# Two parked expert groups per query tile, half weight tiles, a tenth row buffer and 85 parked groups in a one-core encoder block

## The chip, the cores and the metric

The kernel runs on one core of one Trainium2 chip. A core has a matrix engine (TensorE, in the profile PE, with its weight loads as PEld), VectorE (DVE), ScalarE (ACT), GpSimd (POOL) and SyncE (SP), which here only issues DMAs. Each engine works through its own queue in order; they meet at semaphores. The metric is the device time of one execution in microseconds (us).

## What is computed

One layer of an encoder on 1024 tokens of width 1024: attention and a bidirectional state-space mixer, merged by gates, and then an expert mixer (PEER) with 16384 experts. The change lies in the expert mixer:

```python
def peer(h, w_query, keys1, keys2, u_tab, v_tab):
    ...
        q = (xt @ w_query).reshape(T, PEER_HEADS, 2, PEER_D_HALF)
        s1 = jnp.einsum('thd,hkd->thk', q[:, :, 0], keys1).astype(jnp.float32)
        s2 = jnp.einsum('thd,hkd->thk', q[:, :, 1], keys2).astype(jnp.float32)
        v1, i1 = lax.top_k(s1, PEER_TOPK)
        v2, i2 = lax.top_k(s2, PEER_TOPK)
        cand = (v1[..., :, None] + v2[..., None, :]).reshape(...)
        sc, pos = lax.top_k(cand, PEER_TOPK)
        idx = jnp.take_along_axis(cidx, pos, axis=-1)
        g = jax.nn.softmax(sc, axis=-1)
        u = u_tab[idx]
        a = jax.nn.gelu(jnp.einsum('thkd,td->thk', u, xt).astype(jnp.float32))
        vv = v_tab[idx]
        return jnp.einsum('thk,thkd->td', (g * a).astype(vv.dtype), vv)
```

Every token picks 128 experts (8 heads of 16), takes the dot product of each expert's row of `u` with the token, a gelu and a gate, and adds up the same experts' rows of `v`.

## The kernel before

The kernel does the expert mixer in two ways at once. For the first `TB` = 384 tokens (three blocks of 128) it **fetches** the picked rows: `rows` (L1162) issues an indirect DMA from POOL that brings one row of 1024 numbers for each of 128 tokens into a buffer `br`; a row of `u` is met by a dot product on DVE (`dot`, L1189), four of `v` by matmuls with a diagonal of weights (`add`, L1229). For the other `TA` = 640 tokens it computes **all experts densely**: the 128 groups of 128 experts each give a hidden tile `a`, gelu of `u` group times tokens (`hidden_parts`, L1303), which is multiplied by a gate tile that is zero where an expert was not picked, and then by the group's rows of `v` (`mixed`, L1560).

All products of the dense part are made in three matmuls from a high and a low half of each operand (`mm3`, L192). `weights` (L178) loads a weight tile in two raw halves `wr` (three buffers, DMA from SP), casts each on ACT into `wh` and subtracts on POOL into `wl`. `wh` and `wl` are tiles of 8 x 128 columns with two buffers each. With a list `late`, the subtracts are put off until `lows` is called; for a while in the routing `halves_by` sends them to DVE.

The stages of the expert half, with their times in the profiled execution:

1. Query loop (L1421, from about 1420 us): for 16 query tiles, PE multiplies the later tokens by a slice of `w_query`, scores them against the keys, and then runs four parts, that is one tile, of `parking`: it computes the hidden tile of one group ahead of its gate and writes it to DRAM (`a_d`). Meanwhile DVE takes the top 16 of each score tile (`top`, five passes) and routes the first three blocks (`route`). As soon as the first block is routed (`early`), fetches begin.
2. The rest of the tops and routes (L1441 to L1463, to about 2150 us). `hide` runs parked parts on PE while DVE has planned work ahead, up to `4 * NPARK - HOLD` parts.
3. Placing (L1482, to about 2582 us): DVE compares indices four tokens at a time (`quad`, `GB` = 6 buffers), PE multiplies them into gate tiles, which go to DRAM (`G_d`). `hide` goes on parking.
4. The last loop (L1594, to about 4000 us): the 128 groups in 43 lots of `EG` = 3. For each lot the hidden tiles are computed or, if parked, read back from DRAM; they are multiplied by the gate tile (`weigh`), and the lot before is mixed.

The order of the instructions on PE, DVE and POOL in these stages is written out by the program as it runs (`manual`), on ACT and SP a scheduler chooses it. The program keeps three planned clocks, `at_pe`, `at_dve` and `at_dma`: `follow` and `hide` give work to the engine that is behind, and `feed` (L1356) issues row fetches until `at_dma` has caught up with the larger of the other two. Each fetch adds 1.6 to `at_dma`; a u row adds 1.25 to `at_dve`, a v row 0.46 to `at_pe`.

The fetches have `NROW` = 9 row buffers. `drain(keep)` (L1168) puts the dots or matmuls of earlier rows into their queues until at most `keep` rows are open, and then the next fetch is issued; `keep` is `NROW - 1`.

88 of the 128 groups are parked, spread evenly, so most lots hold two parked groups, two hold three, and the computed one may stand at any place in its lot.

`hidden_parts` goes through its two token halves j one after the other, with eight slices kd each; the refill of its weight tile is ordered at the end (`load`), and the subtracts of the refill ordered before are put in at the middle:

```python
        for j in range(NJ):
            ...
            for kd in range(8):
                mm3(o, (uh[:, kd], ul[:, kd]), (h2h[kd][:, js], h2l[kd][:, js]), kd == 0, kd == 7)
                done += 1
                if done == 4 * NJ:
                    lows()
                if done % (2 * NJ) == 0 and done < 8 * NJ:
                    yield None
            ACT.activation(a[:, js], o, AF.Gelu_apprx_tanh)
        load()
        yield a
```

Of the kernel before, what the change touches and what calls it, by code (L numbers as in the profile page):

```python
# [28 lines left out]
W2 = TA // NJ  # L29
CUTS = [(0, TQ)] + [(TQ + j * W2, W2) for j in range(NJ)]  # L30
EPS = 1e-6
NEG = -3.0e38
EG = 3
NPARK = 88
BSTEP = 3
FSTEP = 2
NROW = 9
VG = 4
# [9 lines left out]
NGQ = 2  # L48
GB = 6
RDVE = 1  # L50
# [8 lines left out]
NSTG = 2  # L59
WH = 2  # L60
WL = 2
VB = 3
# [56 lines left out]
def block(ctx, tc, A, out, dbg=None):  # L119
# [57 lines left out]

    def weights(src, kd, eng=None, late=None):  # L178
        hi = wp.tile([128, 8, 128], FR, name="wh", bufs=WH)
        lo = wp.tile([128, 8, 128], FR, name="wl", bufs=WL)  # L180
        for k in range(0, kd, 4):
            raw = wp.tile([128, 4, 128], F32, name="wr", bufs=WR)
            nc.sync.dma_start(raw, src[:, k:k + 4])
            if late is None:
                split(raw, hi[:, k:k + 4], lo[:, k:k + 4], eng and eng[k // 4])
                continue
            ACT.copy(hi[:, k:k + 4], raw)  # L187
            late.append(lambda k=k, raw=raw: ((eng and eng[k // 4]) or POOL).tensor_tensor(  # L188
                lo[:, k:k + 4], raw, f32(hi[:, k:k + 4]), op=OP.subtract))
        return hi, lo  # L190
# [605 lines left out]
    bidx = bp.tile([128, NB, 128], I32, name="bidx")  # L796
    bg = bp.tile([128, NB, 128], F32, name="bg")
    hx = pool("hx")
    la = pool("la")
# [155 lines left out]
    rt = pool("rt", "right")  # L955
    kr = rt.tile([128, N_KR], F32, name="kr")
    nc.sync.dma_start(kr, A["kr"])
    for nm, x in zip("hl", (xh, xl)):
        for p, a in zip(x, others(nm, FR)):
            p[1] = a  # L960
    h2h, h2l = ([x[m][1] for m in range(8)] for x in (xh, xl))
    ip = pool("ip", "right")
    bw = pool("bw", "right")
    best = [bw.tile([128, 4, 2, 8, 16], F32, name="best", bufs=2) for _ in range(2)]
    where = [bw.tile([128, 4, 2, 8, 16], U32, name="where", bufs=2) for _ in range(2)]
# [68 lines left out]
    def route(blk):  # L1034
# [66 lines left out]
        if blk < NB:  # L1101
            V.tensor_copy(bidx[:, blk], exf)
            V.tensor_copy(bx[:, blk], exf)
            V.tensor_copy(bg[:, blk], gf)
            ready.append(blk)
            yield
            return
        ei = T([128, 3, 128], "ri3", I32)
# [18 lines left out]
    def final(p, src, t0, n, x1):  # L1127
        tl = slice(t0, t0 + n)
        nc.sync.dma_start(x1, x1_d[:, :, tl])
        yield "w"  # L1130
        yield "w"
        yield "w"
        for m in range(8):
            V.scalar_tensor_tensor(x1[:, m], src[:, m // 4, m % 4], mod[:, 40 + m:41 + m], x1[:, m], op0=OP.mult, op1=OP.add)
        yield "w"
        o = wide()
        acc = o[:, 0]
        for m in range(0, 8, 2):
            some = []
            for _ in range(2):  # L1140
                some.append(p.tile([128, n], F32, name="fsq", bufs=2))
# [12 lines left out]
        nc.sync.dma_start(out[:, :, tl], x1)  # L1154

    def fetched():
# [5 lines left out]
        def rows(tab, idx):  # L1162
            r = rt.tile([128, D], F32, name="br", bufs=NROW)
            POOL.indirect_dma_start(out=r, out_offset=None, in_=A[tab],  # L1164
                                    in_offset=bass.IndirectOffsetOnAxis(ap=idx, axis=0))
            return r
# [5 lines left out]
        for b in range(NB):  # L1172
# [3 lines left out]
            aT = rt.tile([128, 128], F32, name="aT")  # L1176
            yield from drain(NROW - 1)
            st = rt.tile([128, D], F32, name="br", bufs=NROW)
            nc.sync.dma_start(st, h2t_d[b])
            hrow = []  # L1180
# [16 lines left out]

            def weights_of(b=b, a=a, aT=aT):
                ACT.activation(a, a, AF.Gelu_apprx_tanh)
                yield "w"  # L1200
                V.tensor_tensor(a, a, bg[:, b], op=OP.mult)
                yield "w"
                yield "w"
                yield "w"
                o = P1()
                PE.transpose(o[:, :128], a, ident)
                ACT.copy(aT, o[:, :128])

            ahead.append((1, begin))
            for s in range(128):  # L1210
                yield from drain(NROW - 1)
                r = rows("u", bidx[:, b, s:s + 1])
                ahead.append((1, lambda s=s, r=r, dot=dot: dot(s, r)))
                if s == 96:
# [5 lines left out]
            def add(i, R, aT=aT, acc=acc):  # L1220
                if not acc:
                    acc.append(wide())
                z = zb[i // VG % 2]
                if i % VG == 0:
                    ACT.copy(z[:, :, 31:31 + 32 * VG:32], aT.rearrange("p (g i) -> p g i", g=4)[:, :, i:i + VG])
                at = 31 + 32 * (i % VG) - i
                for h in range(2):
                    for g in range(4):
                        PE.matmul(acc[0][32 * g:32 * g + 32, h], lhsT=z[:, g, at:at + 32], rhs=R[g][:, h * 512:(h + 1) * 512],  # L1229
                                  start=(i == 0), stop=(i == 31))  # L1230
                return
                yield

            def finish(b=b, acc=acc):
                s = rt.tile([128, D], F32, name="bacc")
# [5 lines left out]
                for m in range(8):  # L1241
                    PE.transpose(o[:, m // 4, m % 4], s[:, m * 128:(m + 1) * 128], ident)
                x1 = rt.tile([128, 8, 128], F32, name="bacc")
                yield from final(rt, o, b * 128, 128, x1)

            for i in range(32):
                R = []
                for g in range(4):
                    yield from drain(NROW - 1 - g)
                    R.append(rows("v", ixt[:, 32 * g + i:32 * g + i + 1]))  # L1250
                    yield "v"
# [24 lines left out]
    lt.release()  # L1276
    la.release()
    dn = pool("dn")
# [13 lines left out]

    def load():
        lows()
        src = next(sources, None)
        if src is not None:
            loaded.append(weights(src, 8, halves_by, late))

    load()
    load()  # L1300
    lows()

    def hidden_parts(c):  # L1303
        uh, ul = loaded.popleft()
        a = dn.tile([128, TA], F32, name="a", bufs=2)
        done = 0
        for j in range(NJ):
            o = psE.tile([128, 512], F32, name="hb", bufs=2)[:, :W2]
            js = slice(j * W2, (j + 1) * W2)
            for kd in range(8):  # L1310
                mm3(o, (uh[:, kd], ul[:, kd]), (h2h[kd][:, js], h2l[kd][:, js]), kd == 0, kd == 7)
                done += 1
                if done == 4 * NJ:
                    lows()
                if done % (2 * NJ) == 0 and done < 8 * NJ:
                    yield None
            ACT.activation(a[:, js], o, AF.Gelu_apprx_tanh)  # L1317
        load()
        yield a

# [100 lines left out]
    for m in range(17):  # L1421
# [15 lines left out]
        if m < 16:  # L1437
            for _ in range(4):
                parked_part()
# [189 lines left out]
    for m in range(8):  # L1629
        x1 = rt.tile([128, TA], F32, name="br", bufs=NROW)  # L1630
        nc.sync.dma_start(x1, x1_d[:, m, TB:])
# [3 lines left out]
    def last(m, j, js, o):  # L1635
        x = acc[:, m, js]
        V.scalar_tensor_tensor(x, o, mod[:, 40 + m:41 + m], x, op0=OP.mult, op1=OP.add)
        sq = rt.tile([128, W2], F32, name="br", bufs=NROW)
        ACT.activation(sq, x, AF.Square)
# [12 lines left out]
    d2.release()  # L1652
    dn.release()
    hx.release()
    bp.release()
# [63 lines left out]
```

## Time and profile before

| | |
|---|---|
| three runs | 4056.01, 4068.97 and 4076.5 us, median 4068.97 |
| the profiled execution | 4056.31 us |
| its span, from first to last instruction | 4054.5 us |
| mean granted PE clock | 0.953 |
| moved by DMA | 854.04 MB, mean 211 GB/s |
| row fetches | 384 of u and 384 of v, 402.70 MB on POOL's queue |
| hidden tiles | 128, of 48 matmuls (128x128 by 128x320) each |

The page gives for each engine the time in which it ran instructions; for a stage, a table by stretches gives the same with the clock that PE was granted. A stage whose PE column is short of its length has PE waiting, and the list of waits names the instruction that waited and the one that released it. A line like `wl L188 <- ACT wh L187` reads: the instruction of line 188 that writes `wl` stood idle until ACT's instruction of line 187 was done. SP's own timeline shows when each DMA was issued.

### The profile page before, as it was taken

The page shows a single profiled execution, that of the slowest core. Times are in us where ns is not written, and L with a number is a line of the kernel's source. Part 1 is how long each engine was busy: PE and PEld are TensorE (multiplying, and loading weights), DVE is VectorE, ACT ScalarE, POOL GpSimd, SP SyncE. Part 2 cuts the span into 40 slices and gives each one's busy share as a digit, 9 for nine tenths or more (in the row PEclk, how much of TensorE's full clock was granted, in tenths as well). Part 3 has the DMA queues.
Part 4 walks back from the last instruction along what each step waited for, and adds up shares of the span by engine and source line. Part 5 has one row for each costly group of instructions (what it writes and reads, how often), then busy time and mean ns, then how long its engine had stood idle before and what let it go on. Part 6 is the DMA issues. An engine that isn't in the chain of part 4 may idle for free.

```text
span 4054.5 us, 61036 instructions
## 1 busy us (share of the span) xinstructions
PE 3660.2 (90%) x22927; PEld 3204.8 (79%) x22927; DVE 2578.8 (64%) x5316; ACT 1339.1 (33%) x2659; POOL 1812.5 (45%) x1529
## 2 busy tenths in 40 slices
PE   5799999998899899679888888999999899999998
PEld 4577777776688799678677788999788899978887
DVE  5698951347672678934785556489444698864456
ACT  4265542223323432122225655422222222222222
POOL 3211112565454567736776545444444343434420
PEclk8899999998899999789998999999999999999999
DMA  5111124323375349944776777888898798889962
GB/s 182 37 46 46 50 89 142 109 92 121 116 231 175 104 165 318 346 164 148 252 250 209 269 270 273 313 284 297 315 315 309 251 314 284 298 293 318 312 231 87
DMA packets 387784, 854.04 MB, mean 211 GB/s; under 512 B 32800, under 2 KB 146976, under 8 KB 384672
## 3 DMA queue, kind: packets, MB, share of 16 engines
q1 hardware_dynamic: 276896, 447.44, 32.5%
q0 software_dynamic: 110592, 402.70, 28.6%
q8 instruction: 180, 2.95, 0.3%
q14 instruction: 116, 0.95, 0.1%
HBM read 740.44 MB, written 109.58 MB: 210 GB/s over the span
## 4 chain that ended last, share of the span: by engine, by line
PE 33%; DVE 9%; DMA 8%; issue 2%; ACT 2%; POOL 2%; SPq 0%; ACTq 0%; POOLq 0%; DVEq 0%
PE pb L195 4%; PE pb L194 4%; PE pb L196 4%; PE hb L194 4%; DMA vr<-v 4%; PE hb L196 4%; PE gx L1229 4%; PE hb L195 4%; PE pb L1346 3%; DVE br L1189 3%; DMA G_d<-stg 2%; PE io L194 1%; PE io L195 1%; DVE Wl L1545 1%; PE io L196 1%
## 5 line engine op out<-in xcount | busy, mean ns | idle before, releaser
L196 PE MATMUL hb<-ah,wl 128*128 128x320 f32 x2048 | 649.3, 317 | 59.5 <-POOL wl L188 41.1
L194 PE MATMUL hb<-ah,wh 128*128 128x320 f32 x2048 | 661.1, 323 | 19.3 <-ACT a L1317 19.1
L195 PE MATMUL hb<-al,wh 128*128 128x320 f32 x2048 | 646.4, 316 | 0.0
L1164 POOL DMA_INDIRECT br<-u,bidx x384 | 366.5, 955 | 470.0 <-DVE br L1189 330.1
L1164 POOL DMA_INDIRECT br<-v,ixt x384 | 381.1, 992 | 425.9 <-PE gx L1229 303.4
L174 POOL TENSOR_TENSOR wl<-wr,wh 128x512 fp32r<-128x512 f32 x170 | 230.0, 1367 | 673.1 <-ACT wh L173 617.7
L194 PE MATMUL pb<-Wh,vh 128*128 128x320 f32 x1536 | 473.6, 315 | 16.3 <-ACT Wh L1542 11.8
L195 PE MATMUL pb<-Wl,vh 128*128 128x320 f32 x1536 | 479.0, 313 | 9.5 <-DVE Wl L1545 9.4
L196 PE MATMUL pb<-Wh,vl 128*128 128x320 f32 x1536 | 476.3, 311 | 0.0
L1189 DVE SCALAR_TENSOR_TENSOR br<-br,gx 128x1024 f32<-128x1024 f32 x384 | 454.9, 1215 | 30.3 <-DMA br<-u,bidx 27.7
L196 PEld LDWEIGHTS hb<-ah,wl 128*128 128x128 f32 x2048 | 396.8, 194 | 67.3 <-POOL wl L188 45.1
L194 PEld LDWEIGHTS hb<-ah,wh 128*128 128x128 f32 x2048 | 398.2, 194 | 48.9 <-issue 24.0
L188 POOL TENSOR_TENSOR wl<-wr,wh 128x512 fp32r<-128x512 f32 x269 | 343.2, 1296 | 201.2 <-ACT wh L187 198.7
L195 PEld LDWEIGHTS hb<-al,wh 128*128 128x128 f32 x2048 | 397.8, 194 | 0.0
L1575 DVE TENSOR_TENSOR acc<-acc,pb 128x320 f32<-128x320 f32 x492 | 229.8, 485 | 209.1 <-PE pb L196 207.8
L187 ACT CAST wh<-wr 128x512 fp32r<-128x512 f32 x288 | 177.1, 618 | 560.4 <-DMA wr<-uT 303.9
L173 ACT CAST vh<-vr 128x512 fp32r<-128x512 f32 x256 | 150.9, 618 | 614.1 <-PE pb L195 395.1
L194 PEld LDWEIGHTS pb<-Wh,vh 128*128 128x128 f32 x1536 | 288.1, 190 | 43.5 <-ACT Wh L1542 16.7
L195 PEld LDWEIGHTS pb<-Wl,vh 128*128 128x128 f32 x1536 | 290.7, 189 | 17.7 <-DVE Wl L1545 14.2
L1331 DVE TENSOR_TENSOR quad<-io,rig 128x1024 f32<-128x1024 f32 x160 | 190.4, 1221 | 166.6 <-PE pb L1346 105.1
L196 PEld LDWEIGHTS pb<-Wh,vl 128*128 128x128 f32 x1536 | 290.4, 189 | 0.2
L194 PE MATMUL w<-hh,wh 128*128 128x512 f32 x560 | 230.1, 411 | 8.2 <-ACT zg L548 4.3
(362 smaller groups left out, 8235.6 us busy)
## 6 DMA issues: line engine op xcount, KB each, us to landing
wr<-uT SPq DMA_DIRECT2D x256, 256.0 KB, 4.5
vr<-v SPq DMA_DIRECT2D x256, 256.0 KB, 5.7
G_d<-stg SPq DMA_DIRECT2D x20, 2048.0 KB, 12.2
gt<-G_d SPq DMA_DIRECT2D x42, 960.0 KB, 6.5
a_d<-a SPq DMA_DIRECT2D x88, 320.0 KB, 4.4
a<-a_d SPq DMA_DIRECT2D x88, 320.0 KB, 5.9
wr<-wi SPq DMA_DIRECT2D x82, 256.0 KB, 2.7
sq<-adaT SPq DMA_DIRECT2D x32, 512.0 KB, 4.3
```

The costliest lines, as they stand in the source:

```text
L173: ACT.copy(hi, src)
L174: (eng or POOL).tensor_tensor(lo, src, f32(hi), op=OP.subtract)
L187: ACT.copy(hi[:, k:k + 4], raw)
L188: late.append(lambda k=k, raw=raw: ((eng and eng[k // 4]) or POOL).tensor_tensor(lo[:, k:k + 4], raw, f32(hi[:, k:k + 4]), op=OP.subtract))
L194: PE.matmul(o, lhsT=wh, rhs=xh, start=first, stop=False)
L195: PE.matmul(o, lhsT=wh, rhs=xl, start=False, stop=False)
L196: PE.matmul(o, lhsT=wl, rhs=xh, start=False, stop=last)
L1164: POOL.indirect_dma_start(out=r, out_offset=None, in_=A[tab], in_offset=bass.IndirectOffsetOnAxis(ap=idx, axis=0))
L1189: V.scalar_tensor_tensor(v2(r), v2(r), 1.0, hrow[0], op0=OP.mult, op1=OP.mult, accum_out=a[:, s:s + 1])
L1229: PE.matmul(acc[0][32 * g:32 * g + 32, h], lhsT=z[:, g, at:at + 32], rhs=R[g][:, h * 512:(h + 1) * 512], start=(i == 0), stop=(i == 31))
L1331: V.tensor_tensor(x, iota.unsqueeze(1).unsqueeze(1).to_broadcast([128, 2, 4, 128]), ig[:, 0:2, t:t + 4].unsqueeze(3).to_broadcast([128, 2, ...
L1575: V.tensor_tensor(acc[:, m, js], acc[:, m, js], o, op=OP.add)
```

## The change

```diff
-NPARK = 88
-NROW = 9
+NROW = 10
+SLACK = 2
-GB = 6
+GB = 5
-WH = 2
-WL = 2
+WH = 4
+WL = 4
-PARKED = [c for c in range(128) if (c + 1) * NPARK // 128 > c * NPARK // 128]
+PARKED = [c for c in range(128) if c % EG]
+NPARK = len(PARKED)
...
-    def weights(src, kd, eng=None, late=None):
-        hi = wp.tile([128, 8, 128], FR, name="wh", bufs=WH)
-        lo = wp.tile([128, 8, 128], FR, name="wl", bufs=WL)
+    class Halves(list):
+        def __getitem__(self, at):
+            return list.__getitem__(self, at[1] // 4)[:, at[1] % 4]
+
+    def weight_half(src, k, hi, lo, eng=None, late=None):
+        raw = wp.tile([128, 4, 128], F32, name="wr", bufs=WR)
+        nc.sync.dma_start(raw, src[:, k:k + 4])
+        h = wp.tile([128, 4, 128], FR, name="wh", bufs=WH)
+        w = wp.tile([128, 4, 128], FR, name="wl", bufs=WL)
+        hi.append(h)
+        lo.append(w)
+        if late is None:
+            split(raw, h, w, eng)
+            return
+        ACT.copy(h, raw)
+        late.append(lambda: (eng or POOL).tensor_tensor(w, raw, f32(h), op=OP.subtract))
+
+    def weights(src, kd):
+        hi, lo = Halves(), Halves()
         for k in range(0, kd, 4):
...
+            weight_half(src, k, hi, lo)
         return hi, lo
...
-            r = rt.tile([128, D], F32, name="br", bufs=NROW)
+            r = rg.tile([128, D], F32, name="br", bufs=NROW)
...
-                yield from drain(NROW - 1)
+                yield from drain(NROW - 1 - SLACK)
...
-                    yield from drain(NROW - 1 - g)
+                    yield from drain(NROW - 1 - SLACK - g)
...
-    sources = [x for m in range(16) for x in (A["wq"][m], A["uT"][order[m]])] + [A["uT"][c] for c in order[16:]]
+    sources = [x for m in range(16) for x in (A["wq"][m], A["uT"][order[2 * m]], A["uT"][order[2 * m + 1]])]
+    sources += [A["uT"][c] for c in order[32:]]
...
-    def load():
-        lows()
-        src = next(sources, None)
-        if src is not None:
-            loaded.append(weights(src, 8, halves_by, late))
-
+    def load(half=None):
+        if half != 1:
+            src = next(sources, None)
+            if src is not None:
+                loaded.append((Halves(), Halves()))
+                coming.append(src)
+        for k in (0, 1) if half is None else (half,):
+            lows()
+            if coming:
+                weight_half(coming[0], 4 * k, *loaded[-1], halves_by and halves_by[k], late)
+                if k:
+                    coming.pop()
...
-        for j in range(NJ):
-            o = psE.tile([128, 512], F32, name="hb", bufs=2)[:, :W2]
...
+        turn[0] = NJ - 1 - turn[0]
+        first = [abs(turn[0] - j) for j in range(NJ)]
+        o = {}
+        parts = [(j, k) for k, js in ((0, first), (1, first[::-1])) for j in js]
+        for n, (j, k) in enumerate(parts):
+            if not k:
+                o[j] = psE.tile([128, 512], F32, name="hb", bufs=2)[:, :W2]
             js = slice(j * W2, (j + 1) * W2)
...
+            for kd in range(4 * k, 4 * k + 4):
+                mm3(o[j], (uh[:, kd], ul[:, kd]), (h2h[kd][:, js], h2l[kd][:, js]), kd == 0, kd == 7)
+            if k:
+                ACT.activation(a[:, js], o[j], AF.Gelu_apprx_tanh)
+            if n in (0, 2):
+                lows()
+            if n in (1, 3):
+                load(n // 2)
+            yield a if n == 3 else None
...
-            for _ in range(4):
+            for _ in range(8):
                 parked_part()
                 follow(0.0)
```

The weight tiles become two half tiles each, with four buffers in place of two whole ones, so the bytes are the same. A hidden tile is computed in four parts of 12 matmuls: the first four slices kd for both token halves, and then the last four, in the opposite order of the halves. Each half of the weight tile is ordered anew as soon as both token halves are through with it. The query loop parks two groups per query tile. Of every three groups the first is computed in the last loop and the other two are parked, 85 in all. The row buffers are ten and lie in a pool of their own on the other side of the memory; a fetch is issued when at most seven rows are open. `kr`, a constant, moves to a pool that is released earlier, and the placing has five buffers in place of six.

The rest of the diff (`TH`, `half`, `hidx`, `hg`, new `CUTS`, views in `final` and `add` for a block of 64 tokens) is for a `TB` that is not a multiple of 128; `TB` stays 384 here.

More of the change, by code (lines that the diff above doesn't have):

```diff
@@ L29 @@
 W2 = TA // NJ
-CUTS = [(0, TQ)] + [(TQ + j * W2, W2) for j in range(NJ)]
+TH = TB % 128
+CUTS = [(0, TQ)] + [(t, min(512, (S - TQ) // -(-(S - TQ) // 512))) for t in range(TQ, S, (S - TQ) // -(-(S - TQ) // 512))]
 EPS = 1e-6
@@ L797, in block @@
     bg = bp.tile([128, NB, 128], F32, name="bg")
+    if TH:
+        hidx = bp.tile([128, 64], I32, name="hidx")
+        hg = bp.tile([128, 64], F32, name="hg")
     hx = pool("hx")
@@ L960, in block @@
             p[1] = a
+            if TH:
+                (ACT.copy if nm == "h" else POOL.tensor_copy)(a[:, :TQ - TB], f32(p[0])[:, TB:])
     h2h, h2l = ([x[m][1] for m in range(8)] for x in (xh, xl))
@@ L1104, in route @@
             V.tensor_copy(bg[:, blk], gf)
+            if TH and blk == NB - 1:
+                for src, dst in ((bidx, hidx), (bg, hg)):
+                    nc.sync.dma_start(dst[0:64], src[0:64, blk, 0:64])
+                    nc.sync.dma_start(dst[64:128], src[0:64, blk, 64:128])
             ready.append(blk)
             yield
-            return
+            if not TH or blk < NB - 1:
+                return
         ei = T([128, 3, 128], "ri3", I32)
@@ L1176, in fetched @@
             aT = rt.tile([128, 128], F32, name="aT")
-            yield from drain(NROW - 1)
-            st = rt.tile([128, D], F32, name="br", bufs=NROW)
-            nc.sync.dma_start(st, h2t_d[b])
+            yield from drain(NROW - 1 - SLACK)
+            st = rg.tile([128, D], F32, name="br", bufs=NROW)
+            half = 128 * b + 128 > TB
+            if half:
+                for k in range(2):
+                    nc.sync.dma_start(st[64 * k:64 * k + 64], h2t_d[b, 0:64])
+            else:
+                nc.sync.dma_start(st, h2t_d[b])
+            at_idx, at_g = (hidx, hg) if half else (bidx[:, b], bg[:, b])
+            slots = 64 if half else 128
             hrow = []
@@ L1205, in weights_of @@
                 o = P1()
-                PE.transpose(o[:, :128], a, ident)
-                ACT.copy(aT, o[:, :128])
+                if half:
+                    PE.transpose(o[0:64, :128], a, ident)
+                    for k in range(2):
+                        ACT.copy(aT[64 * k:64 * k + 64, 0:64], o[0:64, 64 * k:64 * k + 64])
+                else:
+                    PE.transpose(o[:, :128], a, ident)
+                    ACT.copy(aT, o[:, :128])
             ahead.append((1, begin))
-            for s in range(128):
-                yield from drain(NROW - 1)
-                r = rows("u", bidx[:, b, s:s + 1])
+            for s in range(slots):
+                yield from drain(NROW - 1 - SLACK)
+                r = rows("u", at_idx[:, s:s + 1])
                 ahead.append((1, lambda s=s, r=r, dot=dot: dot(s, r)))
-                if s == 96:
+                if s == slots - 32:
                     flipped()
@@ L1218, in fetched, with add @@
             acc = []
-            def add(i, R, aT=aT, acc=acc):
+            steps = 16 if half else 32
+            def add(i, R, aT=aT, acc=acc, steps=steps):
                 if not acc:
@@ L1242, in finish @@
                     PE.transpose(o[:, m // 4, m % 4], s[:, m * 128:(m + 1) * 128], ident)
[L1243 to L1246 removed]
+                x1 = rt.tile([128, 1024], F32, name="bacc")[:, :8 * n].rearrange("p (m t) -> p m t", m=8)
+                yield from final(rt, o, b * 128, n, x1)
+            for i in range(steps):
                 R = []
                 for g in range(4):
[L1249 to L1250 removed]
+                    yield from drain(NROW - 1 - SLACK - g)
+                    R.append(rows("v", ixt[:, steps * g + i:steps * g + i + 1]))
                     yield "v"
```

50 lines of the change are left out of this document (20 added, 30 removed).

## The prediction

> **What bounds the kernel now.** I read the page first. TensorE (PE) is busy for 90% of the span, so time can only be won where PE stands still, and the other engines matter where they make it stand.
>
> ```profile
> PE 3660.2 (90%) x22927; PEld 3204.8 (79%) x22927; DVE 2578.8 (64%) x5316; ACT 1339.1 (33%) x2659; POOL 1812.5 (45%) x1529
> ```
>
> Second, the table by stretches, cut at the stages of the expert half: the query loop, the routing, the placing, and the last loop over 43 groups. Columns: length, busy time and instructions of each engine, granted clock, DMA share, GB/s.
>
> ```profile
> 1420.00:1610.00 190.00, 188.53 (x1309) 188.06 (x1310) 159.50 (x657) 59.95 (x127) 129.81 (x115) 1.00 0.68 237
> 1610.00:1760.00 150.00, 88.15 (x522) 86.57 (x521) 134.91 (x442) 25.56 (x53) 96.75 (x97) 0.77 0.84 318
> 1760.00:1900.00 140.00, 136.35 (x914) 136.09 (x913) 32.43 (x114) 38.91 (x79) 64.32 (x50) 0.98 0.38 128
> 1900.00:2150.00 250.00, 216.02 (x1385) 174.52 (x1384) 184.89 (x574) 59.51 (x114) 199.85 (x155) 0.94 0.75 245
> 2150.00:2582.00 432.00, 378.22 (x2789) 353.79 (x2788) 250.41 (x280) 249.02 (x758) 232.00 (x220) 0.92 0.73 263
> 2640.00:2860.00 220.00, 206.65 (x1370) 202.18 (x1369) 190.15 (x336) 54.55 (x97) 87.23 (x86) 0.99 0.88 295
> 2860.00:3180.00 320.00, 317.52 (x2190) 259.88 (x2189) 152.36 (x254) 67.45 (x123) 148.76 (x145) 1.00 0.90 314
> 3260.00:3620.00 360.00, 339.40 (x2219) 324.08 (x2219) 303.37 (x539) 84.84 (x151) 144.76 (x143) 0.99 0.88 297
> ```
>
> The first row is a full PE at full clock: 188.5/1309 = 0.144 us per matmul. At that rate the 2745 matmuls of the first three rows are 395 us of work in 480 us. So some 82 us are lost (with 0.145 for the rounding), and 74 of them in the second row (150 - 522 x 0.145), where the clock is down to 0.77 besides. The fourth row loses 49 us the same way (34 of them idle), the fifth has 54 us idle, the two stretches with u rows in the last loop (sixth and eighth) lose 22 and 39.
>
> Third, who stops PE in the second row. The waits between 1600 and 1720:
>
> ```profile
> ACT wh L187 <- DMA wr<-uT: 44.5, 4, 15.3
> PE pb L196 <- POOL wl L188: 32.9, 3, 15.7
> ```
>
> PE waits for the low half of a weight tile (`wl`, POOL), ACT for a raw weight half (`wr`). The timeline of SP's queue shows why the raw half is late, and POOL's shows what POOL did meanwhile:
>
> ```profile
> 1608.12 0.33 SPq L183 DMA_DIRECT2D wr<-uT  x1
> ...
> 1635.34 0.33 SPq L183 DMA_DIRECT2D wr<-uT  x1
> ```
> ```profile
> 1608.23 0.95 POOL L1164 DMA_INDIRECT br<-u,bidx  x1
> ...
> 1633.08 0.94 POOL L1164 DMA_INDIRECT br<-u,bidx  x1 [0.31 <-DVE best L995]
> 1634.04 3.74 POOL L188 TENSOR_TENSOR wl<-wr,wh 128x512 fp32r<-128x512 f32 x3
> ```
> ```profile
> DMA to landing us min/median/max: 2.6/5.4/6.3
> ```
>
> For 27 us no weight half is issued, since the three `wr` buffers wait for `wl`, and in POOL's queue 21 row fetches of 1.24 us stand ahead of it. The transfer itself lands in 5.4 us (third row, `wr` between 1590 and 1780). So this loss is one of order in POOL's queue, not of DMA speed.
>
> The burst comes from the planner (L1356 to L1440). Followed through with its constants, the query loop issues 6 or 7 u rows per query tile up to m = 11, then 21, 14, 14 and 26 for the last four: the left-over tops and u rows drive `at_dve` to 317 while `at_pe` is at 232, and every step of `at_dve` buys fetches. Between two `wl` stand up to 21 fetches, as in the trace.
>
> **The change, part by part.** `TB` stays 384, so `TH` is 0 and everything under `if TH` or `half` does nothing; `CUTS` gives the same three cuts. That is 0.
>
> *Two parked groups per query tile.* PE's planned time per query tile grows from 14.5 to 21.4 and DVE's work stays under it: `at_dve` ends the loop at 342.5, as `at_pe` does. The rows come at 7 to 11 per tile, and at most 7 stand between two `wl`. Real PE time per tile is (48 + 96) x 0.144 = 20.7 us and some 2 us of scores. POOL: 6 `wl` of 1.30 and 9 fetches of 1.24, 19 us. DVE: 9 dots and 5 tops of five passes:
>
> ```profile
> L1189 DVE SCALAR_TENSOR_TENSOR br<-br,gx 128x1024 f32<-128x1024 f32 x384 | 454.9, 1215 | 30.3 <-DMA br<-u,bidx 27.7 <-ACT gx L1184 2.2
> L1189 DVE DVE_READ_ACCUMULATOR br<-br,gx 128x1 f32 x384 | 32.2, 84 | 0.0
> L997 DVE MAX8 best<-st 128x8 f32<-128x128 f32 x128 | 36.8, 288 | 2.7
> ```
>
> That is 9 x 1.30 + 25 x 0.288 = 19 us, a little more with route steps. All lie under PE's 22.7, but not far. Before has 100 us with the same mix and rate:
>
> ```profile
> 1500.00:1600.00 100.00, 98.57 (x689) 98.30 (x688) 89.76 (x315) 29.16 (x66) 75.45 (x71) 1.00 0.90 314
> ```
>
> PE held 98.6% there. I charge 2% of the 350 us loop and 8 us for the 60 us behind it: 15 us lost in place of 82, a gain of **67** (25 if the balance is too tight, 75 if nothing is lost). 16 groups leave the routing stage; their PE time is only moved.
>
> *Half weight tiles, four buffers, and the new order of the hidden parts.* Same bytes, same instructions. A part is 12 matmuls, 1.73 us. Before, the whole tile is refilled at its end, the `wl` are written two parts later and read two parts after that. Now half 0 is refilled after the second part, its `wl` written one part later and read six parts after the refill order: 8 to 10 us of room in place of 3.5. The stalls this aims at, in the routing stage and the placing:
>
> ```profile
> PE hb L196 <- DVE wl L188: 17.2, 7, 5.5
> PE hb L196 <- POOL wl L188: 9.6, 9, 1.9
> ```
> ```profile
> PE hb L196 <- POOL wl L188: 8.6, 1, 8.6
> ```
>
> Of 27 us in routing I take 15 (0 to 27: DVE is in order, and the subtract now waits on PE one part earlier, with the route steps behind it), of 8.6 in placing 5 (0 to 9): **20**. What is late next in routing is DVE's wait for POOL's `ro`, which stays. The early stages use `weights` too, but the one wait of PE for a weight between 1100 and 1420 is this:
>
> ```profile
> PE pb L196 <- POOL wl L174: 1.8, 1, 1.8
> ```
>
> So 0, from -10 to +10 as the order on ACT may shift.
>
> *Ten row buffers, two kept free.* POOL may issue a fetch while the dot two places back is unfinished. In the last loop it waits for dots most of all:
>
> ```profile
> POOL br L1164 <- DVE br L1189: 332.2, 162, 9.8
> ```
>
> But PE is not behind that wait, DVE and the DMA are; 0, at best 20 of the 61 us lost in the u stretches. Tiles moved between pools (`kr`, `br`) cost nothing that a wait shows.
>
> *85 parked, `GB` 5.* Three tiles more are computed in the last loop and three less ahead: 0 for PE, and 6 transfers of 320 KB fewer. But the limit `4*NPARK - HOLD` falls from 344 to 332 parts. Before reaches only 331 in the placing. After reaches 332 some 15 quads before its end; from there PE has only placements, while the planner, with PE short, buys 33 u rows for DVE.
>
> ```profile
> L1331 DVE TENSOR_TENSOR quad<-io,rig 128x1024 f32<-128x1024 f32 x160 | 190.4, 1221 | 166.6 <-PE pb L1346 105.1 <-issue 26.2 <-ACT quad L1340 11.1
> L1346 PE MATMUL pb<-quad 128*128 128x128 f32 x1280 | 171.7, 290 | 37.0 <-ACT stg L1349 28.7 <-POOL quad L1337 8.4
> ```
>
> DVE: 15 x 1.22 + 33 x 1.30 = 61 us. PE: 15 x 171.7/160 = 16 us. Until then PE is the slower (quads wait 105 us for it), so DVE may be up to four quads of 432/160 = 2.7 us ahead: 45 less 11 is 34, plus 16/0.77 - 16 = 5 for the clock as in the second row of the stretches. I take **+40** (15 to 61). The 38 rows more that are done by then are missing later, where the two u stretches lose 61 us over 72 + 121 rows (0.32 each): **-12** (0 to -20).
>
> ```profile
> 2640.00:2860.00 220.00, 69.55 (x72) 0.99 0.88 295
> 3260.00:3620.00 360.00, 116.39 (x121) 0.99 0.88 297
> ```
>
> One quad buffer less: 0 (to +8, the one wait of PE for a late quad). Behind the placing 8 parts are left in place of 21, so the first mix has 16 parts (28 us) of cover for the write of `G_d`, `gt` and three weighings, where it had 29: **+3** (0 to 10).
>
> A sentence on the clock: the Trainium skill (TensorE: Matmul & The Clock Gate, Part 1) says that an idle window of about 3.4 us halves the PE clock. In the tail of the placing a quad comes every 4 us, so by that rule its 16 us of matmuls would take 32, and the sum would be 11 us worse. The trace's mean of 0.77 over a starved stretch lies between; no number above or below uses the rule.
>
> Sum: -67 - 20 + 40 - 12 + 3 = **-56 us**. The profiled execution took 4056.3 (span 4054.5), the lowest of the runs shown; their median is 4069.0. So 4000 for such an execution, and **4013** on the scale of the median, which I forecast (1.4% faster).
>
> **Rivals.** (a) *Slower: the gelu behind a late weight.* Both `hb` banks are now open through a tile, and a bank is free only when ACT's gelu follows within one part (1.73 us) instead of two. ACT stands in order behind casts that wait for weights; in routing:
>
> ```profile
> ACT wh L187 <- DMA wr<-uT: 64.6, 14, 9.8
> ```
>
> 14 waits of 4.6 us, each 2.9 beyond a part: 41 us on some 20 tiles. At half that rate over 85 parked tiles it is 87 us, and the result 4013 + 87 = **4100**. It decides from 0.9 us per parked tile ((56 + 20)/85). Against it: a `wr` buffer is now freed five parts ahead of its use (8.7 us, over the 5.4 of landing), where every second half had two. Chance 0.13.
>
> (b) *The gathers crowd the query loop.* Per tile 6 x 256, 2 x 320 and 9 x 512 KB are 6.9 MB; at the 314 GB/s above that is 22.1 us against PE's 22.7. If the rate is the 237 to 263 of the neighbouring rows it is 26 to 29 us, up to 60 to 100 us in the loop; with the rows then slipping out of it, some 50: **4063**. For it: 0.90 of DMA already; against it: 318 GB/s at 0.84 in the very next row. The Trainium skill (DMA: Bandwidth & Descriptors, Issuing engines are not separate DMA queues) holds that queues of all engines share the same 16 DMA engines, so a weight half would queue among gathers; the 5.4 us landing shows little of that. Chance 0.14.
>
> (c) *The halves do nothing for PE and the tail costs its upper end*: -67 + 61 - 12 + 10 = -8, **4061**. The clock of the placing speaks for it (0.92 with gaps already). Chance 0.12.
>
> **How the numbers follow.** Forecast 0.61 with its own range 3975 to 4045 (gain terms each at three quarters, or all at their better ends). The low end 3950 is -75 - 36 + 15 - 20 = -116; the high end 4090 takes in (b), (c) and most of (a). About 0.5% (20 us) is what a measurement of this kernel can tell from no change. Faster by more: 0.61 and a little of (b) and (c), 0.66; within: 0.20; slower: 0.14.
>
> **What would show it.** Right: no stretch of the query loop under 95% PE, at most 7 fetches between two `wl`, the routing begins about 65 us earlier, PE's waits for `wl` under 15 us in all; at the end of the placing some 50 us with PE near a third and DVE full. Wrong: PE waiting for `a` (L1317) at the start of tiles by tens of us (a), or PE in the query loop waiting for `wr` while POOL is free (b); no gap at the end of the placing would make it better than forecast.

## The result, and the profile after

The changed kernel took 4006.3 us (median of four runs, 4000.5 to 4008.1) against 4065.1 us for the kernel before beside it (4056.0 to 4076.5). The ratio is 0.9846, with a 95% interval from 0.9823 to 0.9868. A second set of runs, below, gave 0.988 (0.9859 to 0.9901). Both intervals lie under 1: the kernel is faster, by 1.2 to 1.5%. Forecast were 4013 us and 1.4%, so the sum was right. Two of its terms were not, and that their errors cancelled is luck.

The engine totals of the page after say little: TensorE does the same 22927 matmuls and is busy for 91% in place of 90%.

The table by stretches says more. It is cut here at the same points of the work: query loop, routing, placing, the stretch up to the first full mix, last loop. First the kernel before, then the changed one, which has its query loop in two rows. Columns as in the prediction.

```profile
1420.00:1900.00 480.00, 413.03 (x2741) 410.71 (x2742) 326.85 (x1212) 124.41 (x259) 290.88 (x260) 0.92 0.64 230
1900.00:2143.00 243.00, 210.12 (x1347) 168.96 (x1347) 179.24 (x562) 58.55 (x112) 194.36 (x150) 0.94 0.75 244
2143.00:2575.00 432.00, 379.61 (x2805) 355.11 (x2804) 253.60 (x288) 248.64 (x757) 236.22 (x225) 0.92 0.73 261
2575.00:2640.00 65.00, 57.02 (x363) 55.71 (x362) 24.00 (x36) 24.15 (x49) 29.75 (x27) 0.95 0.85 306
2640.00:4055.00 1415.00, 1343.99 (x9196) 1204.39 (x9194) 938.41 (x1659) 324.75 (x588) 531.46 (x521) 0.98 0.82 279
```
```profile
1420.00:1785.00 365.00, 359.49 (x2469) 358.58 (x2470) 287.33 (x1068) 115.04 (x232) 264.88 (x237) 1.00 0.80 281
1785.00:1830.00 45.00, 34.01 (x223) 28.68 (x221) 41.46 (x128) 9.41 (x22) 31.80 (x27) 0.89 0.68 228
1830.00:2089.00 259.00, 231.22 (x1495) 185.41 (x1495) 197.03 (x614) 66.50 (x123) 209.18 (x163) 0.95 0.77 251
2089.00:2530.00 441.00, 377.77 (x2783) 359.29 (x2782) 284.90 (x343) 253.61 (x760) 259.25 (x249) 0.92 0.77 279
2530.00:2600.00 70.00, 44.76 (x266) 42.82 (x264) 32.91 (x50) 22.18 (x45) 23.87 (x21) 0.80 0.83 297
2600.00:3999.00 1399.00, 1338.19 (x9245) 1211.54 (x9244) 901.18 (x1581) 325.33 (x589) 509.72 (x488) 0.98 0.78 268
```

A stretch's loss is its length less its matmuls times 0.145 us, the measure of the prediction. It is a better ledger than the busy time, since a matmul at a lower clock counts as loss too.

| stretch | lost before | lost after | change | predicted |
|---|---|---|---|---|
| query loop | 82.6 | 7.0 + 12.7 | -63 | -67 |
| routing | 47.7 | 42.2 | -5 | -15 (halves) |
| placing | 25.3 | 37.5 | +12 | +40 and -5 (halves) |
| up to the first full mix | 12.4 | 31.4 | +19 | +3 |
| last loop | 81.6 | 58.5 | -23 | -12 |
| sum | | | -60 | -56 |

The hidden parts begin 6 us later than before (1433.7 against 1427.7), and 29 matmuls more, 4 us, lie behind 1420, so the spans differ by 56 us (3998.6 against 4054.5).

Who stops PE? These are PE's waits on a weight's low half (`wl`) and on gelu (`a`) over the whole trace, before and then after. Columns: us in all, times, longest. The fourth row of before, 32.9 us on `pb`, stands in the prediction.

```profile
PE hb L196 <- POOL wl L188: 41.1, 13, 14.0
...
PE hb L194 <- ACT a L1317: 19.1, 6, 7.5
PE hb L196 <- DVE wl L188: 18.3, 8, 5.5
```
```profile
PE hb L205 <- ACT a L1369: 25.5, 9, 5.9
```

The 92 us of waits for `wl` are gone by name, and the wait for gelu is longer by 6. (One idle time of 9 us in the placing stands ahead of an `hb` matmul that reads `wl` and has no releaser in the profile; it may be of the same kind.) POOL's timeline in the query loop shows the other side: where up to 21 fetches stood between two `wl`, there are five in the stretch below, and seven at most in the whole loop, as forecast.

```profile
1607.49 1.30 POOL L195 TENSOR_TENSOR wl<-wr,wh 128x512 fp32r<-128x512 f32 x1 [0.79 <-ACT wh L194]
1608.94 0.95 POOL L1192 DMA_INDIRECT br<-u,bidx  x1
...
1614.04 0.94 POOL L1192 DMA_INDIRECT br<-u,bidx  x1 [0.30 <-issue]
1614.98 1.32 POOL L195 TENSOR_TENSOR wl<-wr,wh 128x512 fp32r<-128x512 f32 x1
```

In the routing the gelu waits come from ACT's order. Its timeline has the exp of a route step (L1090) waiting 13.6 us for DVE's subtract (L1089), with a load of 1.28 us of ACT's tables on either side, and the next gelu (L1369) behind it. Four of PE's waits, 15.8 of the 25.5 us, end with the gelu behind such an exp.

```profile
1911.27 1.28 ACT L1090 ACT_TABLE_LOAD   x1
1926.20 0.31 ACT L1090 ACTIVATE rg<-rg 128x128 f32<-128x128 f32 x1 [13.64 <-DVE rg L1089]
...
1927.04 1.28 ACT L1369 ACT_TABLE_LOAD   x1
```

The end of the placing in slices of 10 us shows the gap that the prediction described, though PE is near a third only at worst (70% over the 50 us); DVE is nearly full with the u rows that the planner bought.

```profile
2480.00:2490.00 10.00, 6.21 (x37) 5.95 (x36) 8.44 (x14) 3.36 (x12) 7.07 (x7) 0.83 1.01 420
2490.00:2500.00 10.00, 10.00 (x75) 9.87 (x74) 7.58 (x11) 5.54 (x16) 4.85 (x5) 1.00 1.02 407
2500.00:2510.00 10.00, 7.91 (x54) 7.19 (x52) 10.00 (x17) 4.26 (x14) 6.08 (x7) 1.00 1.03 411
2510.00:2520.00 10.00, 3.43 (x16) 2.94 (x16) 10.00 (x16) 2.25 (x8) 8.28 (x9) 0.67 1.02 401
2520.00:2530.00 10.00, 7.35 (x28) 6.47 (x29) 7.94 (x13) 4.26 (x14) 8.12 (x10) 0.50 0.97 351
```

It loses 50 - 210 x 0.145 = 20 us. Behind it the first mix waits for `Wh`, which waits in the end for transfers. The waits between 2530 and 2600:

```profile
PE pb L205 <- ACT Wh L1599: 24.4, 3, 20.9
...
ACT wh L194 <- DMA wr<-uT: 13.6, 1, 13.6
```

### The profile page after: what moved, and what is told of

Same layout as the page of the kernel before. It is cut to its first block, busy times and chain, and to the rows that moved or that the text cites. A ratio compares the mean times of both kernels' runs of the same rounds, so it can differ in the third digit from the quotient of the medians.

```text
span 3998.6 us, 61125 instructions
## 1 busy us (share of the span) xinstructions
PE 3633.1 (91%) x22927; PEld 3188.4 (80%) x22927; DVE 2601.3 (65%) x5316; ACT 1357.6 (34%) x2658; POOL 1828.6 (46%) x1529
## 5 line engine op out<-in xcount | busy, mean ns | idle before, releaser
L205 PE MATMUL hb<-ah,wh 128*128 128x320 f32 x2048 | 653.4, 319 | 25.5 <-ACT a L1369 25.5
L207 PE MATMUL hb<-ah,wl 128*128 128x320 f32 x2048 | 641.0, 313 | 9.6 <-issue 9.6
L195 POOL TENSOR_TENSOR wl<-wr,wh 128x512 fp32r<-128x512 f32 x269 | 352.5, 1316 | 394.6 <-ACT wh L194 364.6
L176 POOL TENSOR_TENSOR wl<-wr,wh 128x512 fp32r<-128x512 f32 x170 | 232.1, 1369 | 634.9 <-ACT wh L175 455.6
L176 DVE TENSOR_TENSOR vl<-vr,vh 128x512 fp32r<-128x512 f32 x256 | 198.5, 776 | 80.9 <-ACT vh L175 70.0
```

Source lines behind the costliest of these rows:

```text
L176: (eng or POOL).tensor_tensor(lo, src, f32(hi), op=OP.subtract)
L195: late.append(lambda: (eng or POOL).tensor_tensor(w, raw, f32(h), op=OP.subtract))
L205: PE.matmul(o, lhsT=wh, rhs=xh, start=first, stop=False)
L207: PE.matmul(o, lhsT=wl, rhs=xh, start=False, stop=last)
```

## The experiments

All ratios are to the kernel before, run beside each kernel on the same chip. 0.001 is 4 us. The changed kernel's own two ratios lie 14 us apart, so a difference of that size between sets of runs on different chips is not told from nothing. "Whole" means weight tiles in one piece, "nine rows" nine row buffers with none kept free, "ten rows" ten with two kept free.

### Two groups or one

The changed kernel with one parked group per query tile:

```
-    sources = [x for m in range(16) for x in (A["wq"][m], A["uT"][order[2 * m]], A["uT"][order[2 * m + 1]])]
-    sources += [A["uT"][c] for c in order[32:]]
+    sources = [x for m in range(16) for x in (A["wq"][m], A["uT"][order[m]])] + [A["uT"][c] for c in order[16:]]
...
-            for _ in range(8):
+            for _ in range(4):
                 parked_part()
```

> The changed kernel, but one parked group per query tile again. If the gain is the order of the row fetches in the query loop (my term of 67 us), the bursts of 21 and 14 fetches between two weight subtracts come back, the last four query tiles lose some 60 to 70 us of PE, and the whole is 50 to 70 us slower than the changed kernel: 4050 to 4075. If the half weight tiles are what helps (they give a weight half 8 to 10 us of room), the burst does less harm and it stays under 4030. One thing goes the other way in both: the planner then ends the placing without running out of parked parts (176 u rows fetched by then, not 213), so the gap there should be gone, some 15 to 40 us of it, and 4030 to 4050 with a burst would still fit the first theory; the query loop's PE column decides.

And the kernel before with that edit the other way round, and nothing else of the change:

> The kernel before with nothing but two parked groups per query tile: whole weight tiles, nine row buffers, 88 parked, spread. Order theory: the 74 us lost around 1610 to 1760 go, the placing does not run out of parts (344, the limit, is just reached at its end), so 55 to 75 us faster than before: 3990 to 4010, as good as the whole change. Half-tile theory: with the weights just as late as before the loop stays starved and the gain is under 25 us: 4040 or more.

Measured were 0.9958 (0.9946 to 0.9969) without the two groups, and 0.988 (0.9858 to 0.9902) with them alone, 49 us. The stretch from 1420 to 1760 of the query loop, first with one group and then with two alone, and PE's wait for the `wl` of the queries with one group:

```profile
1420.00:1760.00 340.00, 282.89 (x1863) 280.34 (x1861) 297.11 (x1118) 88.64 (x181) 229.57 (x212) 0.92 0.76 277
```
```profile
1420.00:1760.00 340.00, 330.23 (x2249) 327.61 (x2249) 253.98 (x952) 101.72 (x212) 235.22 (x212) 0.99 0.77 270
```
```profile
PE pb L207 <- POOL wl L195: 31.4, 3, 13.2
```

With one group the burst is back, 31.4 us of PE's waits as in the kernel before (32.9), although the half tiles and the ten rows are there. 340 - 1863 x 0.145 = 70 us are lost in this stretch. With two groups alone 14 are lost. So the two groups are what ends the burst, and alone they bring 49 of the whole change's 49 to 63 us: the other three edits together are worth 0 to 14. Both runs missed their expected time. Two groups alone were to bring 55 to 75 us. Without them the kernel is 32 to 46 us slower than the whole change, not 50 to 70: its placing does not run out of parts, as the expectation allowed, and loses 11 us in place of 33 from its first quad to its last.

### Half tiles

The changed kernel with whole weight tiles and the old order of the hidden parts, first on one chip and then beside the changed kernel on another:

```
-WH = 4
-WL = 4
+WH = 2
+WL = 2
...
-            weight_half(src, k, hi, lo)
+            raw = wp.tile([128, 4, 128], F32, name="wr", bufs=WR)
...
-        for n, (j, k) in enumerate(parts):
+        for j in range(NJ):
```

> The changed kernel with whole weight tiles, refilled at the end of a tile, and the old order of the hidden parts. Prediction's term: the halves are worth 20 us, so 4025 (15 to 30 slower). Rival: PE's waits for weights are exchanged for waits on the gelu behind ACT's queue (25.5 us in the changed kernel, 19.3 before), so within 10 us of the changed kernel. If it is over 50 us slower, the halves carry the gain in the query loop too.

> The changed kernel once more, unaltered, as the measure for the three runs beside it on the same chip. Both theories expect its ratio to the kernel before at 0.9846 give or take 0.002, some 62 us faster.

> The changed kernel with whole weight tiles and the old order of the hidden parts, beside the changed kernel itself. Theory A (the half tiles gain as forecast: 20 us): 20 us slower than the changed kernel, a ratio of about 0.989. Theory B (the half tiles trade waits for weights against waits for gelu and gain nothing): within 5 us of it. Theory C (they cost, as the earlier run's 0.9813 hints): 8 to 15 us faster than the changed kernel, a ratio of about 0.981.

Whole tiles gave 0.9813 (0.9791 to 0.9834) and 0.9811 (0.9796 to 0.9827), and the changed kernel beside the second 0.988 (0.9859 to 0.9901). The half tiles **cost** 28 us on that chip, and 14 against the first measurement of the change. Where is it to be seen? Both profiles of the second pair, cut at the first and the last quad: up to the first quad the half tiles lose 8 us more (63.2 against 54.8), in the placing 4 (37.0 against 33.3), in the 90 us behind it 8 (40.8 against 32.4), in the rest 10 (66.9 against 56.9).

From 1420 to 2100 PE waits 24.3 us for gelu with half tiles and 12.4 with whole ones, and the first quad comes 11 us later (2086.7 against 2075.7). With whole tiles and ten rows PE waits only 16 us for `wl` in this window, so there is little left for the half tiles to remove. PE's waits in the 90 us behind the last quad, half tiles first:

```profile
PE pb L205 <- ACT Wh L1599: 25.7, 4, 20.8
```
```profile
PE pb L196 <- ACT Wh L1577: 9.2, 3, 7.3
PE hb L196 <- ACT wh L189: 6.2, 1, 6.2
```

With half tiles ACT stands up to 13.4 us there for one raw half, with whole ones 8.6. The first pair of profiles shows the same two places (6 and 5 us), but neither of the others: its placing loses 4 us less with half tiles, its last loop 2 more. Two profiles of the changed kernel itself end 15 us apart (spans 3998.6 and 4013.7), 10 of them in the last loop, so what is beyond the two places was not tied to the half tiles.

The half tiles alone, on the kernel before:

> The kernel before with the half weight tiles, their four buffers and the new order of the hidden parts, and nothing else of the change. The prediction: 20 us faster than before (a ratio of 0.995), from waits of PE for weights in the routing and the placing. The rival, from the whole-tile runs (0.981 with whole tiles against 0.988 with halves): slower than before by up to 28 us (1.000 to 1.007), with PE's waits for wl gone from these stages but its waits for ACT's gelu longer by as much.

0.9974 (0.9961 to 0.9987): 11 us faster. The waits from 1420 to 2100, before and with the half tiles:

```profile
PE hb L196 <- POOL wl L188: 30.7, 11, 14.0
PE hb L196 <- DVE wl L188: 13.7, 5, 5.5
PE hb L194 <- ACT a L1317: 12.5, 4, 7.5
```
```profile
PE hb L203 <- ACT a L1334: 57.1, 7, 17.6
```

The 44 us of waits for `wl` on `hb` are exchanged for 45 us more behind gelu (a wait of 7.7 us, ahead of a matmul that reads `wl`, has no releaser in this profile). This is rival (a), at about half its price. The first quad starts no earlier for it (2153.8 against 2146.6); the gain is in the placing, whose last quad starts at 2549.6 against 2554.7. So the same edit gains here and costs there, and the runs with nine rows, below, tell why.

### Exp later

A try to take away ACT's wait for the exp of the route step, once with half tiles and once with whole ones:

```
-        ACT.activation(g, g, AF.Exp)
...
+            if h == 4:
+                ACT.activation(g, g, AF.Exp)
```

> The changed kernel with the exp of the routing step issued on ACT some steps later, when DVE has finished the subtract that it waits for. Theory A (ACT stands 51 us behind that subtract in the routing, gelu behind it, PE behind gelu): the waits of ACT for rg fall from 51 us to under 10, PE's waits for ACT's gelu in the routing from 18 us to under 6, and the time by 8 to 15 us. Theory B (PE then waits for something else of the same step, such as weights): the waits for rg go but the time stays within 4 us.

> Whole weight tiles and the exp later, both. Theory A (the two losses are separate): the gains of both edits add up, 15 to 25 us faster than the changed kernel, a ratio near 0.979. Theory B (the half tiles cost only because gelu stands behind the exp, one part of slack in place of two): whole tiles and half tiles give the same time once the exp is later, within 4 us of the run with the exp later and half tiles.

0.9863 (0.9846 to 0.988) and 0.9802 (0.9788 to 0.9817): 7 and 4 us, within the intervals of 0.988 and 0.9811. ACT's wait for DVE's subtract from 1800 to 2090 is 53.0 us in the changed kernel and 52.6 with the exp later.

The edit missed its aim. ACT's timeline still has gelu, table load and exp in a row: the exp stands in ACT's order, which the scheduler chooses, where it stood. What the wait itself is worth stays untested; the run with both edits repeats that whole tiles are faster.

### Row buffers

The version with whole tiles, with nine row buffers and none kept free:

```
-NROW = 10
-SLACK = 2
+NROW = 9
+SLACK = 0
```

> The changed kernel with whole weight tiles, nine row buffers and none kept free. The version with whole tiles and ten stands at 0.9811, the one with only the two groups at 0.988: 28 us come from the rest. Theory A (they come from the ten row buffers with two kept free, as POOL waits less for dots): back to 0.988, POOL's waits for dots in the last loop up by 80 us or more. The prediction (row buffers 0): stays at 0.981 give or take 0.002.

0.9914 (0.9893 to 0.9934): the row buffers, priced at nothing, are worth 42 us here, more than the 28 that theory A named. POOL's waits for dots in the last loop did not grow by the 80 us that theory A named (251 us from 2600 on, against 226). The 42 us begin in the query loop: the first quad comes 15 us later than with ten rows (2090.4 against 2075.7), the end of the span 34 (4017.4 against 3983.3). Whether the tenth buffer or the two kept free do it was not tested apart. The stretch from 1420 to 1760 with nine rows and with ten, both with whole tiles:

```profile
1420.00:1760.00 340.00, 326.57 (x2218) 323.41 (x2218) 255.69 (x933) 100.44 (x209) 239.71 (x216) 0.99 0.78 273
```
```profile
1420.00:1760.00 340.00, 338.50 (x2336) 337.44 (x2337) 270.72 (x1003) 106.21 (x220) 248.41 (x224) 1.00 0.80 283
```

18 us are lost with nine rows and 1.3 with ten. And the waits from 1420 to 2100 in the same order:

```profile
POOL br L1183 <- DVE br L1215: 40.7, 26, 7.9
PE hb L198 <- POOL wl L190: 24.4, 9, 4.9
PE hb L198 <- DVE wl L190: 14.4, 7, 4.8
```
```profile
POOL br L1183 <- DVE br L1215: 13.3, 14, 4.8
PE hb L198 <- DVE wl L190: 8.4, 5, 2.2
PE hb L198 <- POOL wl L190: 6.9, 2, 6.8
```

With nine rows POOL stands 41 us before a fetch whose buffer's dot DVE has not done, and the `wl` behind that fetch in POOL's order stands too: PE waits 39 us for `wl`, with ten rows 15.

The last run puts half tiles and nine rows together:

> The changed kernel with nine row buffers and none kept free, half tiles kept. With whole tiles the ten row buffers were worth 0.0103 (0.9914 to 0.9811). Theory A (half tiles and row buffers are two cures for the same waits of PE for wl; with nine rows the half tiles still gain, with ten they only cost): 0.988 to 0.991 here, no worse than 0.9914 of whole tiles and nine rows, and PE's waits for wl in the query loop and the routing below half of the 44 us that whole tiles and nine rows show. Theory B (the half tiles cost 20 to 28 us by themselves, whatever the rows): 0.996 to 0.998.

0.989 (0.9875 to 0.9906), theory A. From 1420 to 2100 PE waits for no `wl`, but 27.4 us for gelu.

### Parts for the end of the placing

The changed kernel with seven parked tiles more, 92 in all:

```
-PARKED = [c for c in range(128) if c % EG]
+PARKED = [c for c in range(128) if c % EG or c in (15, 21, 27, 33, 84, 90, 96)]
```

> The changed kernel with seven more parked groups (15, 21, 27, 33, 84, 90, 96, whose lots then hold three parked ones): 92. Parts no longer run out in the placing (346 planned, limit 360) and 22 are left behind it, as before the change. If the loss of some 45 us at the end of the placing and before the first mix is the lack of parts, it goes: 20 to 40 us faster, 3965 to 3985. If the gap is due to the row fetches' transfers (1.0 of DMA there) it stays, and the run is within 10 us of the changed kernel; lots of three without a hidden tile before their mix could cost 2 to 3 us each.

0.9859 (0.9836 to 0.9882), between the two measurements of the changed kernel (0.9846 and 0.988). The 20 to 40 us did not come. Yet the gap is filled; the stretch from 2500 to 2600, and the rest, in the changed kernel and with 92:

```profile
2500.00:2600.00 100.00, 63.45 (x362) 59.42 (x360) 60.85 (x94) 32.96 (x79) 46.35 (x44) 0.78 0.88 324
```
```profile
2600.00:4060.00 1460.00, 1338.19 (x9245) 1211.54 (x9244) 901.18 (x1581) 325.33 (x589) 509.72 (x488) 0.98 0.75 257
```
```profile
2500.00:2600.00 100.00, 90.68 (x610) 88.99 (x610) 49.15 (x72) 38.20 (x86) 53.11 (x48) 0.97 0.90 315
```
```profile
2600.00:4060.00 1460.00, 1311.59 (x8984) 1177.22 (x8982) 913.57 (x1614) 315.50 (x570) 505.15 (x489) 0.98 0.76 262
```

248 matmuls more in the 100 us are 36 us won. But up to the end of the span the changed kernel loses 1398.6 - 9245 x 0.145 = 58 us and this one 1391.7 - 8984 x 0.145 = 89: 31 are given back. Part of the reason is that DVE had worked off u rows in the gap. The instructions of the dots alone, two for each, from 2600 on:

```profile
2600.00:4060.00 1460.00, 196.03 (x328) 0.98 0.75 257
```
```profile
2600.00:4060.00 1460.00, 211.39 (x354) 0.98 0.76 262
```

So 177 dots are left for the last loop in place of 164, and all 13 more stand in its first stretch with dots (2600 to 2710 in the changed kernel, to 2760 with 92), which loses 14 us more. But another 13 us are given back in the stretch behind it, which holds no dot in either kernel:

```profile
2710.00:3065.00 355.00, 351.18 (x2498) 295.91 (x2497) 175.52 (x302) 80.54 (x150) 152.81 (x147) 1.00 0.84 298
```
```profile
2760.00:3145.00 385.00, 372.48 (x2614) 315.34 (x2612) 197.77 (x338) 87.80 (x161) 149.36 (x146) 0.99 0.83 289
```

By the measure that is -7 us (PE is full, and its matmuls there take a little under 0.145) against +6. The dots cannot be the cause of these 13. The other cause that the expectation named, lots of three parked groups with no hidden tile to compute, fits them: PE's losses there come some 60 us apart, and of the lots, some 32 us each, every second one from 5 to 11 has three. That was not tested by itself.

With whole tiles, and the 88 parked tiles of the kernel before:

```
-PARKED = [c for c in range(128) if c % EG]
+PARKED = [c for c in range(128) if (c + 1) * 88 // 128 > c * 88 // 128]
```

> The changed kernel with whole weight tiles and the 88 parked tiles of before in place of 85, two of every three. Theory A (the 28 us come from the row buffers): stays at 0.981, or a little better, since parts run out later at the end of the placing. Theory B (they come from the even spread, one tile to compute in every group of the last loop): back to 0.988, and the last loop 20 us or more longer. The prediction (running out of parts costs 40 us, one twelfth of the tiles more in the last loop nothing): 10 to 20 us better than 0.981.

0.9753 (0.9726 to 0.9779): 24 us better than the 85 with whole tiles by the ratios (14 by the medians, 13 by the two profiles), and the fastest version of all, 3972 us. The gap lost 33 us less (783 matmuls in place of 553 between 2470 and 2600), and the last loop gave back 21.

### The runs side by side

All of these have two groups per query tile. The first row is the kernel before with nothing else, so it also has six quad buffers in place of five.

| tiles | rows | parked | ratio |
|---|---|---|---|
| whole | nine | 88 | 0.988 |
| whole | nine | 85 | 0.9914 |
| half | nine | 85 | 0.989 |
| half | ten | 85 (the change) | 0.9846 and 0.988 |
| half | ten | 92 | 0.9859 |
| whole | ten | 85 | 0.9813 and 0.9811 |
| whole | ten | 88 | 0.9753 |

Half tiles and ten rows each take away the same waits of PE for `wl`. With ten rows the half tiles cost 14 to 28 us; with nine they gain 10, a difference within the spread between chips, but one that the 11 us of the half tiles alone bear out. With whole tiles the rows gain 42, with half ones 4 to 18, hardly more than that spread.

## Why the prediction was right, and where it was not

**Query loop, -67.** Right in place and size: -63. In 365 us PE waits for no weight and loses 7 us. The reason was right in the main, the burst of fetches in POOL's order goes with the two groups. But the two groups alone leave 14 us in the stretch from 1420 to 1760, and with 85 tiles 18, where the whole change leaves 340 - 2296 x 0.145 = 7. Either of the other two edits takes most of the rest: half tiles with nine rows leave 8, whole ones with ten 1.3.

**Half tiles, -20: this term failed.** "Of 27 us in routing I take 15" counted the room that a weight half gains, 8 to 10 us, and that held: no wait for `wl` is left by name (under 15 us was forecast), and 9.6 us ahead of the matmuls that read it have no releaser. What it left at nothing was the other end of the same edit, the gelu that must free its bank within one part; that stood only among the rivals. Alone the edit gains 11 us, and in the kernel as changed it costs 14 to 28.

**Row buffers, 0: failed too.** "PE is not behind that wait" was read from the last loop, where POOL waits longest for dots. In the query loop and the routing a `wl` stands behind the waiting fetch, and there PE does follow. That wait should have been looked up in every stage in which POOL also makes `wl`.

The two together were taken as -20, and the runs show for both together 0.9914 to 0.9846 or 0.988, 14 to 28 us. The sum of the rest was -67 + 40 - 12 + 3 = -36, and whole tiles with nine rows, which leaves just the rest, measured 0.9914, 35 us. This is why 4013 came out near 4006, and it is luck: two errors of opposite sign in two terms that the prediction had not connected.

**Parts run out, +40, -12 and +3.** The gap is there, but not all in its place. Placing and the stretch behind it lose 31 us more than before, against 38 forecast (40 - 5 + 3): 20 us stand at the end of the placing, and the stretch that was priced at 3 loses 19 more. The u rows were priced rightly. 38 fewer were forecast for the last loop and 35 fewer are left (164 dots against 199), all of them out of its first stretch with dots, which loses 110 - 690 x 0.145 = 10 us (2600 to 2710) in place of 21 (2640 to 2860; by 0.145 the two stretches of the prediction lose 21 and 38, not 22 and 39). That is 11 us, 0.33 for each row. The last loop loses another 12 less elsewhere, and no run says why. As an edit, 85 in place of 88 costs 14 us (nine rows, across two chips) to 24 (ten, 14 by the medians), less than the net 31.

**The clock.** The prediction took the mean of 0.77 for the tail, and the five slices above come to 0.80. It falls to a half in two places: at an idle time of 3.79 us (0.51 from 2486 to 2488), and at one of 5.25 us, from where it stays at 0.50 to 2532:

```profile
2510.15 1.35 PE L1403 MATMUL pb<-quad 128*128 128x128 f32 x8 [1.04 <-issue]
2516.75 2.07 PE L1403 MATMUL pb<-quad 128*128 128x128 f32 x8 [5.25 <-issue]
```

The eight matmuls of a quad then take 2.07 us in place of 1.35. By the Trainium skill (TensorE: Matmul & The Clock Gate, Part 1), an idle window of some 3.4 us halves the clock. The trace agrees, and idle times of about 1 us left the clock at full. It was at half for some 20 of the 50 us, so the whole tail was not slowed.

**The rivals.** (a), gelu behind a late weight, came true in small: 25.5 us in all, 6 more than before, and 45 more with the half tiles alone. It was priced by ACT's waits for raw halves; what held ACT longest in the routing was the exp behind DVE. (b), gathers crowding the query loop, fell: 281 GB/s over the 365 us in which PE loses 7. (c) had the halves doing nothing, which is nearer to what they did, but its tail of 61 us did not come, and it too left out the rows.

**What stays open.** Beyond 6 to 8 us up to the first quad and 5 to 8 behind the placing, what the half tiles cost was not placed. What the exp's wait is worth was not tested, since the edit did not move it in ACT's order. Nor was it tested what lots of three parked groups cost, or which half of the row buffers' edit works.

## What to carry to other kernels

When an in-order engine both issues transfers and makes an operand, price every wait of its queue by what stands behind it, stage by stage; the largest total of such a wait need not be where it hurts. Two edits that remove the same wait do not add up, and the second brings only its own cost, so measure each with and without the other. A gap in the busiest engine may cost less than its length, since another engine works ahead in it: filling it gave back 31 of 36 us in one version, though less than half of that in the stretch where that work was missing, and 21 of 33 in another.

## What was not expected of the hardware

At the end of the placing the 16 DMA engines are full (share 1.01 to 1.03) at 401 to 420 GB/s, where the prediction's rows reached 318 at a share of 0.84. Two weight halves that SP issued from 2531.4 on were cast only from 2548.4, and ACT waited 13.6 us for them; in the query loop of before one landed in 5.4 us. At 281 GB/s and a share of 0.80, in the query loop of the changed kernel, PE loses 7 of 365 us, so bandwidth was not its limit. The tables of ACT are loaded anew, 1.28 us, before and after each exp that stands between two gelus in the routing.
